# A gated MLP by seven block products: sums kept as chains in PSUM, inputs in product order, down results added by DMA

## The chip, the core and the metric

The kernel runs on one core of a Trainium2 chip. The core has five engines that run side by side, each in its own order and held back only by semaphores: TensorE (PE) for matmuls, VectorE (DVE), ScalarE (ACT), GpSimd (POOL), and SyncE (SP), which issues DMAs. PSUM, where matmuls leave their sums, has eight banks of 512 fp32 words for each of 128 partitions; SBUF holds everything else on the chip. The metric is the time of one execution on the device in microseconds (us), lower is better.

## The reference

One step of a decoder layer on 1024 prompt tokens and 8 x 4 sample tokens (1056 columns in all): a state-space head group beside a pooling head group, cross-attention to 256 memory tokens, then a gated MLP, then a final norm. The change is in the MLP alone:

```python
h = rmsnorm(x, norm_ffn)
u = h @ w_up                                   # 1024 -> 2 * 2816
u, ffn_new = causal_dwconv(ffn_buf, u, ffn_conv_w, ffn_conv_b)   # width 3, each channel by itself
g, val = jnp.split(u, [D_FF], axis=-1)
x = x + (jax.nn.silu(g) * val) @ w_down        # 2816 -> 1024
```

All is fp32. Each matmul operand is split into a high and a low part (hi = the value rounded to fp32r, lo = value minus hi), and three passes are summed: w hi by x hi, w lo by x hi, w hi by x lo.

## The kernel before

**Order.** Each engine executes its instructions in the order in which the program issues them to it, by a helper class (`InOrder`); all traced rows therefore carry that helper's line, L94 before and L93 after, and are told apart by tile names. Work that is not on TensorE's direct line is spread by generators (`background`), which are moved on one step every so many ticks; a tick comes after each block of matmuls.

**Weights.** `next_unit` hands out units of weights in a fixed list of steps. For each unit ACT makes the high part (tile `wh`) from a loaded tile (`wr` or `ws`) and DVE the low part (`wl`), about two units ahead. Weight sums for the block products (`s1`, `s2`, `s4` and one difference) are made on DVE in `ws` tiles.

**First product of the MLP.** The 44 output tiles of `w_up` form 22 pairs j (gate and value). For a pair the weights are a 2 x 2 block (a11, a12, a21, a22: two output tiles by two input halves) and the tokens are two halves of 528 columns, so that the inputs are b11, b21 (right half, made first) and b12, b22 (left half). In Winograd's form of Strassen's scheme seven products do the work of eight; their inputs are b11, b21, b22 and the sums t1 to t4. A product is 4 input tiles x 3 passes x 2 column halves of 264, 24 matmuls into an `hm` tile of two PSUM banks. Pairs 0 and 1 (`NPLAIN`) are done plainly by eight products each, four of them early (`up_rh`), while the left half's inputs are still being made. For the other 20 pairs each of the seven products has its own `hm` tile, and DVE adds it to the partial sums in SBUF (`plus`, seven adds a pair; tiles `t`, and `q` for b11's product). `hm` has three buffers; two more banks are small tiles (`ms`).

**Inputs.** `inputs_lh` makes the left half's inputs in background: norm, eight scalings, b12's and b22's parts, then for each k the four sums t1 to t4, two of these on POOL, and their low parts on DVE.

**Down projection.** Six groups of three pairs, eight output tiles each: 48 units, each of two halves of 18 matmuls, placed between the products of the next group's pairs (`DOWN_AT`: none in its first pair, one after each product in the second, one in the third). For each half SP loads the running sum from DRAM (`scr_acc`) into `q`, DVE adds the PSUM tile, SP stores it. The last four pairs' down projection comes in the tail.

Of the kernel before, what the change touches and what calls it, by code (L numbers as in the profile page):

```python
# [14 lines left out]
P = 128  # L15
# [41 lines left out]
NPLAIN = 2  # L57
# [3 lines left out]
X_EVERY = 1.3  # L61
X_ON_V = False
# [19 lines left out]
def body(ctx, tc, A):  # L82
# [38 lines left out]
    pms = ctx.enter_context(tc.tile_pool(name="pms", bufs=2, space=bass.MemoryType.PSUM))  # L121
    wide = ExitStack()
    pmm = [None]

    def psum_mode(banks):
        wide.close()
        pmm[0] = wide.enter_context(tc.tile_pool(name="pmm", bufs=6 // banks, space=bass.MemoryType.PSUM))
# [29 lines left out]
    def mstile():  # L157
        return pms.tile([P, 512], F32, tag="ms", name="ms")
# [66 lines left out]
    def paired(j, between):  # L225
# [25 lines left out]
        for n in ("a11", "s2", "s1", "s4", "a21", "a22", "a12"):  # L251
            steps.append(lambda n=n: one(n))
            plains(between.pop(0))
# [6 lines left out]
    for _ in range(2):  # L260
        plains(A["w_up"][2 * j + r, h] for j in range(NPLAIN) for r in range(2) for h in range(2))
    ffn_order = []
    for gi, (j0, j1) in enumerate(JGROUPS):
        for j in range(j0, j1):
# [5 lines left out]
            if j >= NPLAIN:  # L270
                paired(j, [[A["w_dn"][g, m] for g, m in x] for x in mids])
# [1030 lines left out]
    # The first product of the gated MLP goes by 2 x 2 blocks (output tiles of a pair, inputs by halves, tokens by  # L1302
    # halves) in Winograd's form of Strassen's seven products; here come its inputs and their sums.
# [60 lines left out]
    act = {}  # L1364
    xop = {"b11": [(t[:, rh], t[:, lh]) for t in hs[:4]], "b21": [(t[:, rh], t[:, lh]) for t in hs[4:]]}

    XP = V if X_ON_V else G
    bt = []
# [40 lines left out]
    for n in ("b12", "b22", "t1", "t2", "t3", "t4"):  # L1409
        xop[n] = []  # L1410
# [447 lines left out]
```

## Time and profile before

| | before |
|---|---|
| median of 3 runs | 1742.81 us (1742.59 to 1746.6) |
| span of the profiled execution | 1745.0 us |
| TensorE / DVE / ACT / POOL busy | 97% / 68% / 41% / 10% |
| mean granted TensorE clock | 0.991 |
| gated MLP's first block product starts, its last one ends | about 1001 us, 1683 us |
| DMA moved | 242.94 MB |

The span is the time from the first to the last instruction of one profiled execution; it is 2.2 us above the median of the timed runs. Rows of the timeline give start, duration, engine, operation, result<-operands and, in brackets, the idle time ahead of the first and what ended it. Groups of instructions give busy time and mean duration, then the idle time just ahead of them. "hm<-s,wl" is a matmul into an `hm` tile with an input tile `s` and a low weight half.

### The profile page before, as it was taken

The page shows a single profiled execution, that of the slowest core. Times are in us where ns is not written, and L with a number is a line of the kernel's source. Part 1 is how long each engine was busy: PE and PEld are TensorE (multiplying, and loading weights), DVE is VectorE, ACT ScalarE, POOL GpSimd, SP SyncE. Part 2 cuts the span into 40 slices and gives each one's busy share as a digit, 9 for nine tenths or more (in the row PEclk, how much of TensorE's full clock was granted, in tenths as well). Part 3 has the DMA queues.
Part 4 walks back from the last instruction along what each step waited for, and adds up shares of the span by engine and source line. Part 5 has one row for each costly group of instructions (what it writes and reads, how often), then busy time and mean ns, then how long its engine had stood idle before and what let it go on. Part 6 is the DMA issues. An engine that isn't in the chain of part 4 may idle for free.

```text
span 1745.0 us, 30887 instructions
## 1 busy us (share of the span) xinstructions
PE 1685.5 (97%) x12298; PEld 1614.0 (92%) x12298; DVE 1178.4 (68%) x1769; ACT 709.4 (41%) x1160; POOL 181.4 (10%) x301
## 2 busy tenths in 40 slices
PE   8799999999999989999899989999999999999998
PEld 6599998898998889999679979999999999999998
DVE  7755467766856684433653689778686868678786
ACT  6455573444440233222543456334242424233353
POOL 3400000000010210011002232001010101001010
PEclk9899999999999999999999999999999999999999
DMA  8234235554458634412745522443625263444542
GB/s 346 76 104 156 78 68 105 117 124 98 90 179 295 217 111 156 133 43 73 266 158 184 170 65 61 142 157 108 198 72 200 79 193 110 161 138 133 168 137 100
DMA packets 158495, 242.94 MB, mean 139 GB/s; under 512 B 40576, under 2 KB 77568, under 8 KB 158352
## 3 DMA queue, kind: packets, MB, share of 16 engines
q1 hardware_dynamic: 158352, 240.97, 45.0%
q8 instruction: 97, 1.59, 0.4%
q14 instruction: 46, 0.38, 0.1%
HBM read 176.81 MB, written 64.11 MB: 138 GB/s over the span
## 4 chain that ended last, share of the span: by engine, by line
PE 81%; DVE 7%; DMA 6%; ACT 3%; issue 2%; POOL 1%; SPq 0%; DVEq 0%; ACTq 0%; POOLq 0%
PE hm L94 44%; PE mm L94 28%; PE ms L94 7%; DVE s L94 4%; DMA s<-scr_acs 3%; PE mb L94 2%; DVE t L94 1%; ACT s L94 1%; DMA ld<-scr_z 1%; ACT t L94 1%; DVE wl L94 0%; DMA scr_pool<-t 0%; POOL s L94 0%; DVE q L94 0%; DMA ld<-kc 0%
## 5 line engine op out<-in xcount | busy, mean ns | idle before, releaser
L94 PE MATMUL hm<-s,wh 128*128 128x264 f32 x4160 | 679.5, 285 | 0.8 <-ACT wh L94 0.4
L94 PEld LDWEIGHTS hm<-s,wh 128*128 128x128 f32 x4160 | 578.7, 189 | 1.7 <-ACT wh L94 0.6
L94 PE MATMUL mm<-s,wh 128*128 128x352 f32 x2496 | 487.5, 329 | 0.0
L94 PE MATMUL hm<-s,wl 128*128 128x264 f32 x2080 | 425.0, 286 | 8.9 <-DVE wl L94 8.8
L94 PEld LDWEIGHTS mm<-s,wh 128*128 128x128 f32 x2496 | 413.8, 189 | 5.6 <-issue 1.8
L94 PEld LDWEIGHTS hm<-s,wl 128*128 128x128 f32 x2080 | 323.7, 189 | 10.4 <-DVE wl L94 10.4
L94 ACT ACTIVATE wh<-wr 128x512 fp32r<-128x512 f32 (+1 forms) x220 | 133.6, 607 | 443.5 <-PE mm L94 238.6
L94 PE MATMUL mm<-s,wl 128*128 128x352 f32 x1248 | 270.3, 324 | 0.0
L94 DVE TENSOR_TENSOR wl<-wr,wh 128x512 fp32r<-128x512 f32 (+1 forms) x220 | 151.2, 688 | 114.3 <-ACT wh L94 113.9
L94 PEld LDWEIGHTS mm<-s,wl 128*128 128x128 f32 x1248 | 213.5, 189 | 0.4
L94 DVE SCALAR_TENSOR_TENSOR t<-t,par 128x1104 f32<-128x1104 f32 (+4 forms) x132 | 170.4, 1297 | 31.5 <-ACT t L94 30.0
L94 ACT ACTIVATE s<-s 128x512 f32<-128x512 f32 (+5 forms) x147 | 102.9, 711 | 142.4 <-DVE s L94 78.4
L94 ACT ACTIVATE wh<-ws 128x512 fp32r<-128x512 f32 x120 | 75.7, 631 | 196.5 <-PE hm L94 186.1
L94 DVE TENSOR_TENSOR q<-hm,q 128x528 f32<-128x528 f32 x96 | 67.5, 706 | 89.4 <-DMA q<-scr_acc 61.5
L94 DVE TENSOR_TENSOR s<-s 128x512 f32<-128x512 f32 (+6 forms) x97 | 84.6, 884 | 45.4 <-ACT s L94 44.1
L94 POOL COPY fst<-t 128x2 f32<-128x2 f32 x88 | 47.4, 566 | 501.3 <-DVE t L94 487.4
L94 DVE TENSOR_TENSOR t<-hm,t 128x528 f32<-128x528 f32 x100 | 68.7, 704 | 27.4 <-PE hm L94 26.9
L94 PE MATMUL mb<-s 128*128 128x256 f32 (+2 forms) x480 | 80.9, 324 | 4.6 <-DVE s L94 4.6
L94 DVE TENSOR_TENSOR wl<-ws,wh 128x512 fp32r<-128x512 f32 x120 | 82.1, 685 | 2.6 <-ACT wh L94 2.4
L94 PEld LDWEIGHTS mb<-s 128*128 128x128 f32 x480 | 71.6, 191 | 10.6 <-DVE s L94 5.4
L94 ACT ACTIVATE t<-t,par 128x1104 f32<-128x1104 f32 (+4 forms) x60 | 74.5, 1244 | 7.6 <-DVE t L94 3.4
L94 ACT ACTIVATE s<-t 128x1024 fp32r<-128x1024 f32 (+4 forms) x78 | 49.2, 673 | 46.5 <-DVE t L94 37.0
(180 smaller groups left out, 1534.8 us busy)
## 6 DMA issues: line engine op xcount, KB each, us to landing
q<-scr_acc SPq DMA_DIRECT2D x96, 264.0 KB, 3.0
scr_acc<-q SPq DMA_DIRECT2D x96, 264.0 KB, 2.1
ws<-w_up SPq DMA_DIRECT2D x60, 256.0 KB, 2.8
wr<-w_in SPq DMA_DIRECT2D x56, 256.0 KB, 3.0
wr<-w_up SPq DMA_DIRECT2D x36, 256.0 KB, 2.9
wr<-w_dn SPq DMA_DIRECT2D x48, 192.0 KB, 2.7
s<-scr_acs SPq DMA_DIRECT2D x33, 256.0 KB, 5.6
wr<-w_mo SPq DMA_DIRECT2D x32, 256.0 KB, 2.7
```

Of the source, the lines that this page charges most:

```text
L94: i = fn(*args, **kwargs)
```

## The change

All 22 pairs go by the seven products; for the first four (`NEARLY`) the products of b11 and b21 are made early, one product each with its own tile. The products of a pair form two chains: b11, t2, t1 and b22 are added up by TensorE in one `hm` tile (`pa`), t3 and t4 in another (`pb`); only the first product of a chain clears the tile. Partial sums of a chain are copied out by ACT in two halves (`copied`), or, in the first four pairs, by a DVE add with the early product. A product now does all twelve matmuls of one column half before the other. The eight PSUM banks are four `hm` tiles during the MLP and are divided anew before it and after it. The inputs are made in the order in which the products ask for them, all on DVE and ACT. The down result is copied from PSUM by ACT and added to DRAM by an accumulating DMA that POOL issues.

```diff
-NPLAIN = 2
+NEARLY = 4
 ...
-X_EVERY = 1.3
-X_ON_V = False
+X_EVERY = 1.0
 ...
+            pmm[1] = wide.enter_context(tc.tile_pool(name="pms", bufs=small, space=bass.MemoryType.PSUM))
+        pmm[0] = wide.enter_context(
+            tc.tile_pool(name="pmm", bufs=(8 - small) // banks, space=bass.MemoryType.PSUM))
 ...
+            names = ("a11", "s2", "a21", "s1", "s4", "a22", "a12")
+            if j < NEARLY:
+                names = names[1:-1]
+            paired(j, [[A["w_dn"][g, m] for g, m in x] for x in mids], names)
 ...
+    psum_mode(2, 0)
 ...
-        for n, i in (("b12", 0), ("b22", 4)):
-            for k in range(4):
-                scaled(i + k, lh)
 ...
+        for m in (0, 4, 1, 5, 2, 6, 3, 7):
+            scaled(m, lh)
+            yield
+        t2s, w12 = [], []
         for k in range(4):
             a, b = xs[k], xs[4 + k]
-            t1, t2 = [qp.tile([P, TH], F32, tag="q", name="q") for _ in range(2)]
+            V.tensor_tensor(a[:, rh], a[:, lh], a[:, rh], op=ALU.subtract)
+            t2 = qp.tile([P, TH], F32, tag="q", name="q")
+            V.tensor_tensor(t2, b[:, lh], a[:, rh], op=ALU.subtract)
+            w = (stile(F32R), stile(F32R))
+            S.activation(w[0][:, rh], t2, AF.Copy)
+            yield
+            V.tensor_tensor(w[1][:, rh], t2, w[0][:, rh].bitcast(F32), op=ALU.subtract)
+            V.tensor_tensor(b[:, rh], b[:, rh], t2, op=ALU.subtract)
+            w12.append(w)
+            xop["t2"].append((w[0][:, rh], w[1][:, rh]))
+            yield
+        w23 = []
+        for k in range(4):
+            a, b = xs[k], xs[4 + k]
+            V.tensor_tensor(a[:, lh], b[:, lh], a[:, lh], op=ALU.subtract)
+            w = (stile(F32R), stile(F32R))
+            parts(w[0][:, rh], w[1][:, rh], a[:, lh])
+            w23.append(w)
+            xop["t3"].append((w[0][:, rh], w[1][:, rh]))
 ...
-            XP.tensor_tensor(b[:, rh], b[:, rh], t2, op=ALU.subtract)
-            XP.tensor_tensor(a[:, lh], b[:, lh], a[:, lh], op=ALU.subtract)
 ...
+    def product(name, ps, first=True):
 ...
+        for b in range(2):
             for k, (xh, xl) in enumerate(xop[name]):
                 ...
+                    PE.matmul(ps[:, b, :HB], lhsT=w[:, wc], rhs=x[:, b * HB:(b + 1) * HB],
+                              start=(first and k == 0 and pi == 0), stop=(k == 3 and pi == 2), skip_group_check=not first)
+                if k % 2:
+                    tick()
+        return ps
 ...
+    def copied(out, ps):
+        for b in range(2):
+            S.activation(out[:, b * HB:(b + 1) * HB], ps[:, b, :HB], AF.Copy)
 ...
-            S.activation(v2(pre[j][:, (lh, rh)[r]]), plain_product(r, ("b11", "b21")), AF.Copy)
+        t = pre[j] = stile()
+        copied(t[:, lh], product("b11", hmtile()))
+        plus(t[:, rh], product("b21", hmtile()), t[:, lh])
 ...
-        q = qp.tile([P, TH], F32, tag="q", name="q")
-        S.activation(v2(q), product("b11"), AF.Copy)
+        q = pre[j][:, lh] if j in pre else qp.tile([P, TH], F32, tag="q", name="q")
+        if j in pre:
+            mid()
+            pa = product("t2", hmtile())
+        else:
+            pa = product("b11", hmtile())
+            copied(q, pa)
+            mid()
+            product("t2", pa, False)
+        raws2[0] = r0 = ttile()
+
+        def partial(dst):
+            if j in pre:
+                plus(dst, pa, q)
+            else:
+                copied(dst, pa)
+
+        partial(r0[:, e1])
         mid()
-        p = product("t2")
-        r0 = ttile()
-        plus(r0[:, e1], p, q)
+        pb = product("t3", hmtile())
         mid()
-        plus(r0[:, e0], product("t1"), r0[:, e1])
+        product("t1", pa, False)
+        partial(r0[:, e0])
         mid()
-        p = product("b22")
-        r1 = ttile()
-        raws2[0], raws2[1] = r0, r1
-        plus(r1[:, e0], p, r0[:, e0])
+        plus(r0[:, e0], pb, r0[:, e0])
+        product("b22", pa, False)
+        raws2[1] = r1 = ttile()
+        partial(r1[:, e0])
         mid()
-        p = product("t3")
 ...
-        p = product("t4")
-        plus(r0[:, e1], p, r0[:, e1])
+        product("t4", pb, False)
+        plus(r0[:, e1], pb, r0[:, e1])
 ...
         for hf in range(2):
-            t = qp.tile([P, TH], F32, tag="q", name="q")
-            dma(t, scr["acc"][m, hf])
 ...
-            V.tensor_tensor(v2(t), ps[:, :, :HB], v2(t), op=ALU.add)
-            dma(scr["acc"][m, hf], t)
+            t = qp.tile([P, TH], F32, tag="q", name="q")
+            S.activation(v2(t), ps[:, :, :HB], AF.Copy)
+            G.dma_start(scr["acc"][m, hf], t, accum_op=ALU.add)
 ...
     drain()
+    psum_mode(2)
```

TensorE in pair 6, where the product of t1 ends and that of b22 begins (`hm` with its buffer's number; `wh`, `wl` are the weights; "waits" names the engine whose semaphore is waited for). Before, each product has its own tile:

```order
L94 MATMUL hm_10631<-s_10104,wh_10595 128x264 x2
L94 MATMUL hm_10631<-s_10104,wl_10597 128x264 x2
L94 MATMUL hm_10631<-s_10105,wh_10595 128x264 x2
L94 MATMUL hm_10670<-s_9799,wh_10632 128x264 [waits PE_49,Activation_49]
L94 MATMUL hm_10670<-s_9799,wh_10632 128x264
L94 MATMUL hm_10670<-s_9799,wl_10634 128x264 [waits DVE_49]
L94 MATMUL hm_10670<-s_9799,wl_10634 128x264
```

After:

```order
L93 MATMUL hm_11687<-s_9863,wh_11765 128x264
L93 MATMUL hm_11687<-s_9882,wh_11765 128x264
L93 MATMUL hm_11687<-s_9882,wl_11767 128x264
L93 MATMUL hm_11687<-s_9883,wh_11765 128x264
L93 MATMUL hm_11687<-s_9914,wh_11802 128x264 [waits Activation_49]
L93 MATMUL hm_11687<-s_9914,wl_11804 128x264 [waits DVE_49]
L93 MATMUL hm_11687<-s_9915,wh_11802 128x264
```

Before, b22's first matmul goes to another buffer and waits for its weights and for a matmul long ahead; now it goes on in the buffer of t1 (11687) and waits for an ACT instruction. Which one is seen in ACT's order at the same place (`t_11761` and `t_11863` are the pair's result tiles, `s_11795` belongs to the pair before):

```order
L93 ACTIVATE wh_11765<-ws_11608 128x512
L93 ACTIVATE t_11761<-hm_11687 128x264 [waits PE_49,Pool_49]
L93 ACTIVATE t_11761<-hm_11687 128x264
L93 ACTIVATE s_11795<-t_11720 128x1024 [waits DVE_49]
L93 ACTIVATE s_11795<-t_11720 128x32
L93 ACTIVATE wh_11802<-ws_11688 128x512
L93 ACTIVATE wh_11835<-ws_11518 128x512 [waits DMAHW1_49,PE_49]
L93 ACTIVATE t_11761<-hm_11687 128x264 [waits PE_49]
L93 ACTIVATE t_11761<-hm_11687 128x264
L93 ACTIVATE wh_11871<-ws_11548 128x512 [waits DMAHW2_49,Activation_49]
L93 ACTIVATE t_11863<-hm_11687 128x264 [waits PE_49,Pool_49]
L93 ACTIVATE t_11863<-hm_11687 128x264
```

The two copies of t1's sum stand behind the weight parts of the next two units, and the wait of the first of them is for TensorE, that is for the last matmul of t1; b22's matmul waits for the second copy.

DVE while the left half's inputs are made, before (`s`, `q` are inputs and their sums, `par` the norm's gain):

```order
L94 SCALAR_TENSOR_TENSOR s<-s,par 128x528 x2
L94 TENSOR_TENSOR q<-s 128x528
L94 TENSOR_TENSOR s<-s 128x528
L94 TENSOR_TENSOR q<-s,q 128x528
L94 TENSOR_TENSOR s<-s 128x528
L94 TENSOR_TENSOR wl<-wr,wh 128x512 x2
L94 TENSOR_TENSOR s<-q,s 128x528 x2
L94 TENSOR_TENSOR s<-s 128x528 x2
L94 TENSOR_TENSOR q<-s 128x528
L94 TENSOR_TENSOR wl<-wr,wh 128x512
L94 TENSOR_TENSOR q<-s,q 128x528
```

After, the last rows ahead of t2's low weight part, which is the row with `ws`:

```order
L93 TENSOR_TENSOR s<-q,s 128x528
L93 TENSOR_TENSOR s<-s,q 128x528
L93 TENSOR_TENSOR s<-s 128x528 x2
L93 TENSOR_TENSOR q<-s 128x528 x2
L93 TENSOR_TENSOR s<-s,q 128x528
L93 TENSOR_TENSOR s<-q,s 128x528
L93 TENSOR_TENSOR s<-hm,s 128x528
L93 TENSOR_TENSOR wl<-wr,wh 128x512
L93 TENSOR_TENSOR s<-q,s 128x528
L93 TENSOR_TENSOR s<-s,q 128x528
L93 TENSOR_TENSOR s<-s 128x528 x4
L93 TENSOR_TENSOR wl<-ws,wh 128x512
```

Between the first scaling and that row stand 34 DVE instructions: the 8 scalings, 15 steps towards t2, one more sum, 4 steps of t3's inputs, 2 adds of early products and 4 low weight parts. The 12 printed rows are the later 17 of them. Before, the low parts of single inputs come first and the sums `q` are made from then on, with a step on POOL between.

The way of the down results: DVE before, the two halves of one unit,

```order
L94 TENSOR_TENSOR wl_10912<-wr_10821,wh_10910 128x384 [waits DMAHW2_49,PE_49,Activation_49]
L94 TENSOR_TENSOR t_10847<-t_10847,t_10891 128x1104 [waits DVE_49]
L94 TENSOR_TENSOR q_10859<-hm_10861,q_10859 128x528 [waits DMAHW4_49,PE_49]
L94 TENSOR_TENSOR q_10882<-hm_10884,q_10882 128x528 [waits DMAHW5_49,PE_49]
L94 TENSOR_TENSOR s_10929<-t_10847,s_10928 128x1024 [waits Activation_49]
L94 TENSOR_TENSOR s_10929<-t_10847,s_10928 128x32 [waits Activation_49]
L94 TENSOR_TENSOR wl_10951<-ws_10735,wh_10949 128x512
```

and POOL after, in the second pair of a group:

```order
L93 DMA scr_acc_83<-q_10928 128x528 [waits DMAHW1_49,Activation_49]
L93 DMA scr_acc_83<-q_10950 128x528 [waits Activation_49]
L93 DMA scr_acc_83<-q_11007 128x528 [waits Activation_49]
L93 DMA scr_acc_83<-q_11029 128x528 [waits Activation_49]
L93 DMA scr_acc_83<-q_11089 128x528 [waits Activation_49]
L93 DMA scr_acc_83<-q_11111 128x528 [waits Activation_49]
L93 DMA scr_acc_83<-q_11175 128x528 [waits DMASW0_49,Activation_49]
L93 DMA scr_acc_83<-q_11197 128x528 [waits DMASW1_49,Activation_49]
```

DVE waited for the loaded `q` (DMAHW) and for TensorE; now POOL waits for ACT's copy, and from the ninth DMA on for the one eight places earlier (DMASW).

More of the change, by code (lines that the diff above doesn't have):

```diff
@@ L1361, in body @@
     drain()
+    psum_mode(2, 0)
     act = {}
     xop = {"b11": [(t[:, rh], t[:, lh]) for t in hs[:4]], "b21": [(t[:, rh], t[:, lh]) for t in hs[4:]]}
-    XP = V if X_ON_V else G
-    bt = []
+    for n in ("b22", "t1", "t2", "t3", "t4"):
+        xop[n] = []
     def inputs_lh():
@@ L1542, in up @@
         mid()
-        plus(r1[:, e1], product("b21"), q)
+        if j in pre:
+            S.activation(r1[:, e1], pre[j][:, rh], AF.Copy)
+        else:
+            plus(r1[:, e1], product("b21", hmtile()), q)
         ends(1)
```

104 lines of the change are left out of this document (30 added, 74 removed).

## The prediction

> **What bounds the kernel now.** I read the engines' shares first, then the chain of waits, then what TensorE did before, in and after the gated MLP.
>
> ```profile
> span 1745.0 us, 30887 instructions
> PE 1685.5 (97%) x12298; PEld 1614.0 (92%) x12298; DVE 1178.4 (68%) x1769; ACT 709.4 (41%) x1160; POOL 181.4 (10%) x301
> ```
> ```profile
> 1060.36 636.80 PE hm L94 x5178
> 1697.16 2.18 PE ms L94 x12
> ```
> ```profile
> 1061.00:1697.00 636.00, 636.00 (x5177) 635.57 (x5176) 488.73 (x674) 238.17 (x369) 69.52 (x163) 1.00 0.44 138
> ```
>
> From 1060 to 1697 us the chain is one unbroken piece of TensorE: 636.80 us for 5178 matmuls, 123.0 ns each. The window (columns: PE, weight loads, DVE, ACT, POOL, granted clock, DMA share, GB/s) agrees: PE 100% busy at clock 1.00, DVE 77%, ACT 37%. So nothing that frees DVE, ACT or SP there can shorten the stage; only fewer matmuls can, and every wait put before a matmul is added to the end. What may be won elsewhere lies in the stage's start, where TensorE waits:
>
> ```profile
> 1025.89 0.51 PE L94 MATMUL hm<-s,wl 128*128 128x264 f32 x2 [1.62 <-DVE wl L94]
> 1026.24 0.65 PE L94 MATMUL hm<-s,wh 128*128 128x264 f32 x4
> ...
> 1033.22 0.51 PE L94 MATMUL hm<-s,wl 128*128 128x264 f32 x2 [1.43 <-DVE wl L94]
> 1033.56 0.66 PE L94 MATMUL hm<-s,wh 128*128 128x264 f32 x4
> ...
> 1040.39 0.51 PE L94 MATMUL hm<-s,wl 128*128 128x264 f32 x2 [1.03 <-DVE wl L94]
> ...
> 1046.83 0.77 PE L94 MATMUL hm<-s,wl 128*128 128x264 f32 x2 [3.24 <-DVE wl L94]
> 1047.40 1.08 PE L94 MATMUL hm<-s,wh 128*128 128x264 f32 x4
> ...
> 1050.67 0.41 PE L94 MATMUL hm<-s,wl 128*128 128x264 f32 x2
> ...
> 1058.60 0.51 PE L94 MATMUL hm<-s,wh 128*128 128x264 f32 x2 [0.42 <-ACT wh L94]
> 1060.36 0.66 PE L94 MATMUL hm<-s,wl 128*128 128x264 f32 x2 [1.25 <-DVE wl L94]
> 1060.82 1.08 PE L94 MATMUL hm<-s,wh 128*128 128x264 f32 x4
> ```
>
> The bracket is the wait. They sum to 9.0 us (1.62+1.43+1.03+3.24+0.42+1.25), and behind 1046.83 and 1060.36 four matmuls take 1.08 us instead of 0.65, until the rows at 1050.67 and 1064.43 (below) are at full rate again: nearly half of 3.4 and 3.6 us is lost, some 3.4 us. So the start loses **12.4 us**. All but one wait are for a low weight half (wl), which stands on DVE behind the inputs being made.
>
> **Part 1, fewer matmuls.** Before: 8 early products, 8 plain ones, 20 pairs of seven: 156 products of 24 matmuls. After: 8 early, 4 pairs of five, 18 of seven: 154. 48 matmuls × 0.123 = **−5.9 us**, certain, since they leave a stream that is full.
>
> **Part 2, the start.** The inputs' work, before and after, by these rows:
>
> ```profile
> L94 DVE TENSOR_TENSOR s<-s 128x528 fp32r<-128x528 f32 x16 | 10.7, 701 | 0.1
> L94 DVE TENSOR_TENSOR s<-q,s 128x528 fp32r<-128x528 f32 x8 | 8.6, 1119 | 2.9 <-ACT s L94 2.9
> L94 DVE TENSOR_TENSOR q<-s,q 128x528 f32<-128x528 f32 x4 | 5.1, 1264 | 0.0
> ```
> ```profile
> 1034.83 0.68 DVE L94 TENSOR_TENSOR wl<-wr,wh 128x512 fp32r<-128x512 f32 x1
> 1035.43 2.44 DVE L94 TENSOR_TENSOR s<-q,s 128x528 fp32r<-128x528 f32 x2
> ```
> ```profile
> 1034.99 1.71 POOL L94 TENSOR_TENSOR s<-s,q 128x528 f32<-128x528 f32 x1 [0.65 <-DVE q L94]
> ```
>
> The same 528-column subtraction takes 701 ns in one group and 1119 and 1264 in two others, whose rows lie beside a POOL subtraction. With POOL out of it that stretch goes: 8 × 0.42 + 4 × 0.56 = 5.6 us of DVE, plus the 2.9 us that DVE waited. Against this DVE takes over POOL's 8 sums and drops 4 low halves (+4 × 0.62 = 2.5 us; the pitch of such rows is 0.60 to 0.62, as from 1034.83 to 1035.43), and sums weights for two more pairs. More important is what is needed first: the first Strassen product, t2, needs all 8 scaled halves and 15 of the 16 steps behind them, where the plain product needed 4 scaled halves and 4 low ones.
>
> ```profile
> 1001.42 0.71 DVE L94 TENSOR_TENSOR s<-hm,t 128x528 f32<-128x528 f32 x1 [1.76 <-PE hm L94]
> ...
> 1012.76 2.12 DVE L94 SCALAR_TENSOR_TENSOR s<-s,par 128x528 f32<-128x528 f32 x3
> ```
>
> The new change of PSUM pools makes the first MLP matmul wait for the last add from the old pool (1001.42 + 0.71): it starts at about 1002.2 instead of 1001.3, **+0.9**. The scaled halves start 0.9 later, at 1013.7. From there to t2's low weight the new order has 34 DVE instructions (the order rows in the section on the change): 34 × 0.62 = 21.1, so 1034.8. TensorE has done its eight early products, 24 × 0.123 = 2.95 each, and the norm's transposes (about 1) at 1026.7: 8.1 lost. Then t3's inputs and weights, 9 × 0.62 = 5.6 against a product of 2.95: 2.6 more; t1's 6 × 0.62 = 3.7: 0.8 more. Then four times the sum t1→b22 of an early pair, where TensorE waits for one DVE add between two products of one chain: 0.16 + 0.05 + 0.70 + 0.05 = 0.96 (last matmul's drain, handover, add, handover; rows in part 3), 3.8 in all. After: 0.9 + 11.5 + 3.8 = 16.2 against 12.4 before, **+3.8**; I keep nothing for slow clock, though a long wait may bring it. Bounds: if the waits for inputs are only half (early products' weights come in between) −2; if every DVE instruction waits on its ACT copy by as much as the 2.9 us above shows once, +4. With the clock, −6 to +10.
>
> **Part 3, the chains.** From pair 4 on ACT copies a partial sum out of a PSUM tile that the next product then goes on adding to. The copies are queued behind the product's last matmul, and the next product's first matmul behind the second copy. Where other matmuls lie between, this is hidden: b11→t2 has 11 or 36, t2→t1 13 to 36, t3→t4 48. **t1→b22 has none** in the first and third pair of each group and in the last group: 12 places (pairs 5, 6, 8, 9, 11, 12, 14, 15, 17, 18, 20, 21).
>
> ```profile
> 1184.37 1.11 ACT L94 ACTIVATE t<-t 128x1104 f32<-128x1104 f32 x1
> 1185.38 0.59 ACT L94 ACTIVATE q<-hm 128x528 f32<-128x528 f32 x1
> 1185.87 0.62 ACT L94 ACTIVATE wh<-ws 128x512 fp32r<-128x512 f32 x1
> ```
> ```profile
> L94 PE MATMUL hm<-s,wh 128*128 128x264 f32 x4160 | 679.5, 285 | 0.8 <-ACT wh L94 0.4
> ```
> ```profile
> 1686.57 0.42 ACT L94 ACTIVATE t<-t 128x272 f32<-128x272 f32 x1
> ```
> ```profile
> 1064.43 0.41 PE L94 MATMUL hm<-s,wh 128*128 128x264 f32 x2
> ```
> ```profile
> 1064.88 0.61 ACT L94 ACTIVATE t<-hm 128x528 f32<-128x528 f32 x1 [0.94 <-PE hm L94]
> ```
>
> A 528-column copy out of PSUM takes 0.59 and lets the next start 0.49 later; a 272-column one takes 0.42, so two halves about 0.32 + 0.42 = 0.74. A matmul takes 0.285 to its end against 0.123 from start to start, so 0.16 of drain comes first, and a handover from PE to ACT is 0.04 (the last matmul of a product ends at 1064.43 + 0.41 = 1064.84, ACT starts at 1064.88); I take 0.05 for the way back. Price 0.16 + 0.04 + 0.74 + 0.05 = 1.0 us, 12 places: **+12 us**. ACT has little ahead of the copies there: a weight split whose tile is long free. Bounds: 0.6 a place if the halves overlap more, 1.6 if a split (0.62) stands in the way: +7 to +19. What the chains save, four DVE adds a pair, is worth nothing: DVE was not waited for.
>
> **Part 4, down results.** Loads (96) leave SP, the adds leave DVE (96 × 0.706), both off the path. ACT copies the PSUM tile to q and POOL issues the accumulating DMA.
>
> ```profile
> q<-scr_acc SPq DMA_DIRECT2D x96, 264.0 KB, 3.0
> scr_acc<-q SPq DMA_DIRECT2D x96, 264.0 KB, 2.1
> ```
> ```profile
> L94 DVE TENSOR_TENSOR q<-hm,q 128x528 f32<-128x528 f32 x96 | 67.5, 706 | 89.4 <-DMA q<-scr_acc 61.5
> ```
>
> The trace has no accumulating DMA; it both reads and writes 264 KB, so between 2.1 and 3.0 + 2.1 = 5.1 us. In a second pair two of the three q buffers serve the downs, and a copy waits for the DMA two copies earlier. Two copies come per 36 matmuls of down and 24 of product, 60 × 0.123 = 7.4 us. Less the copy's own 0.6 that is 6.8 us for a DMA before ACT waits; TensorE fills one more hm tile meanwhile (18 matmuls, 2.2, less a copy's 0.5), so it waits above 8.5. 5.1 is below both: I cost it at **0**.
>
> **Part 5, small.** The products run one half (bank) through before the other:
>
> ```profile
> 1683.66 13.51 PE L94 MATMUL hm<-s 128*128 128x400 f32 x72
> 1728.67 1.67 PE L94 MATMUL mb<-s 128*128 128x256 f32 x12
> ```
>
> Runs into one bank at 400 columns: (13.51 − 0.16)/72 = 185 ns, 0.464 a column, 122 ns at 264: no loss. At 256 columns in the tail: (1.67 − 0.16)/12 = 126, 130 at 264: +7 ns × 154 products × 24 = +26 at worst. The first rows are many and in the same kind of tile: **+0**. The second change of pools, ahead of the 400-column matmuls, lets them wait for the last product's add, from its end near 1683.6 to
>
> ```profile
> 1684.14 0.70 DVE L94 TENSOR_TENSOR t<-hm,q 128x528 f32<-128x528 f32 x1
> ```
>
> 1684.84: **+1.2** (0 to 2).
>
> **Sum.** −5.9 + 3.8 + 12 + 0 + 0 + 1.2 = **+11.1 us**. The profiled execution is 1745.0 from first to last instruction, 2.2 above the median of the runs, 1742.81; I add the sum to the median: 1753.9, say **1754 us**. Ends: −5.9 − 6 + 7 + 0 = −5 (1738); −5.9 + 10 + 19 + 2 = +25 (1768).
>
> **Rivals.** *A, faster:* DVE's stretch beside POOL is all that the start waits for; without it no input comes late. Place: 1025 to 1060. Price: the 12.4 us go and nothing takes their place: −5.9 − 12.4 + 12 + 1.2 = −5.1, and with a place of part 3 at 0.8, between its lower bound and my value, −7.5: 1735 us. It decides from the point where t2's low weight is ready by 1026.7 instead of 1034.8. For it: the rows of 1119 and 1264 ns. Against: 23 input steps ahead of t2 where 8 were enough. 0.25. *B, within 0.3%:* the copies run beside the drain and the matmuls of the other half, 0.25 a place: −5.9 + 3.8 + 3 + 1.2 = +2, 1745. For it: the first half is complete 12 matmuls earlier. Against: the order lets both copies wait for the product's last matmul. 0.18. *C, slower by DMA:* above 8.5 us per accumulation TensorE waits for q; at 10 us, with 8 pieces of down in 6 groups, 1.5 × 8 × 6 = +72, 1826. For it: loads of scr_acc were what DVE waited for longest before its adds (61.5 us in the row above). 0.08. *D, slower by clock:* short waits make the clock fall; at the 1.7 us lost after the 3.24 wait, 16 places, +27 on the forecast, 1781. Against: after waits of 1.62 and 1.43 the next four matmuls took 0.65. 0.05. Forecast: 0.44.
>
> The Trainium skill, "TensorE: Matmul & The Clock Gate", section "A second HAM failure mode: psum-queue depth-cycling", says that frequent short idling of TensorE between matmul groups makes the clock swing between half and full rate. That speaks against this change and would make D the result; the rows after 1025.89 and 1033.22 show no such fall.
>
> **How the numbers follow.** About 0.3% (5.2 us) is what a measurement of this kernel tells from no change. Faster: 0.22 of A (its rest ends inside 0.3%) and 0.02 from the forecast's low end: 0.24. Same: 0.18 of B, 0.03 of A and 0.02 of the forecast: 0.23. Slower: the rest, 0.53. The range takes in A, B and the forecast's own ends with 5 us beyond them, and leaves out C, D and the outermost of A, under 2 in 10: **1731 to 1773**.
>
> **What would show it.** Part 1: 5424 matmuls of 264 columns in the MLP. Part 2: TensorE's waits between 1025 and 1060, named DVE wl or DVE s, 10 to 16 us, the first at t2; DVE rows of 0.70 with none above 1. Part 3: in the chain of waits, the unbroken PE piece cut at 12 places by ACT t, near 1.0 us each, none at b11→t2. Part 4: the scr_acc DMA under 6.8 us to landing, and ACT waiting for PE, not DMA, before its q copies. Wrong would be a cut every pair, ACT waiting on DMA, or a granted clock below 0.97 between 1100 and 1640.

## The result, and the profile after

The changed kernel takes **1761.47 us** (median of 4 runs, 1761.29 to 1765.65) against 1744.7 us (4 runs, 1742.59 to 1750.22) for the kernel before on the same chip. The ratio is 1.0098, 95% interval 1.0075 to 1.0122: slower by 16.8 us, about 1%, where 11 were forecast. The engines' shares of the profiled execution after:

```profile
span 1759.5 us, 30638 instructions
...
PE 1686.8 (96%) x12250; PEld 1612.8 (92%) x12250; DVE 1081.2 (61%) x1621; ACT 783.8 (45%) x1374; POOL 252.2 (14%) x389
```

TensorE does 48 matmuls less in the program, DVE is freed of 97 us, ACT has 74 us more. What was one piece of TensorE in the chain of waits is now in pieces (start, length, what):

```profile
1095.68 73.21 PE hm L93 x599
...
1169.64 6.11 PE hm L93 x48
...
1182.10 9.06 PE hm L93 x71
...
1191.90 76.34 PE hm L93 x624
...
1268.99 6.11 PE hm L93 x48
```

The waits view of TensorE, first for the start of the MLP (995 to 1102 us), then for the rest of it (1110 to 1700); the numbers are us in total, how often, the longest.

```profile
PE hm L93 <- DVE wl L93: 7.8, 3, 4.1
PE hm L93 <- DVE t L93: 4.7, 4, 1.4
PE hm L93 <- ACT wh L93: 1.5, 2, 0.8
PE hm L93 <- DVE s L93: 0.9, 1, 0.9
```

The last line of it is the first change of pools. Then:

```profile
PE hm L93 <- ACT t L93: 9.2, 12, 0.8
PE hm L93 <- DVE wl L93: 2.5, 6, 0.4
PE hm L93 <- DVE t L93: 1.3, 1, 1.3
```

This second fence is the result in three lines: twelve waits for a copy of a partial sum, six for a low weight half that the prediction did not have, one for the second change of pools. Before, this stretch had no wait at all. The windows view of nearly the same stretch (columns as before) says that nothing else happened to TensorE: it is busy 584.36 of 596.00 us, the 11.6 that are missing are these twelve and six waits (9.2 + 2.5), and the granted clock is 1.00:

```profile
1101.00:1697.00 596.00, 584.36 (x4758) 579.96 (x4756) 336.18 (x431) 291.72 (x546) 147.30 (x241) 1.00 0.50 95
```

To compare kernels I cut every trace at the starts of the same matmuls. *Ahead* runs from TensorE's first matmul to the MLP's first product; *start* ends at pair 4's first product (720 matmuls before, 672 after); *main* ends at the first 400-column matmul (4752 matmuls in all kernels); then the tail, up to the start of TensorE's last matmul. "Lost" is the time between starts of neighbouring matmuls above their usual 0.122 us, counted where the excess is 0.08 us or more; so it takes in the drain ahead of a wait, and slow matmuls: in some runs of four or more they start about 0.22 us apart.

| us | ahead | start (lost) | main (lost) | tail |
|---|---|---|---|---|
| before | 999.8 | 103.8 (16.1) | 578.6 (0) | 54.4 |
| after | 997.6 | 102.4 (20.2) | 597.0 (17.1) | 54.0 |

Main is 18.4 us longer. Its 17.1 are the twelve and the six waits; a last 1.5 is the change of pools, behind the last of its matmuls.

**The twelve.** One of them in the timeline, TensorE and then ACT (start, duration, operation, idle time and its releaser):

```profile
1190.86 0.28 PE L93 MATMUL hm<-s,wh 128*128 128x264 f32 x1
1191.90 0.39 PE L93 MATMUL hm<-s,wh 128*128 128x264 f32 x1 [0.76 <-ACT t L93]
1192.13 0.29 PE L93 MATMUL hm<-s,wl 128*128 128x264 f32 x1
```
```profile
1191.18 0.67 ACT L93 ACTIVATE t<-hm 128x264 f32<-128x264 f32 x2 [1.66 <-PE hm L93]
```

The last matmul of t1 ends at 1191.14, ACT starts 0.04 later, both copies take 0.67, and b22's first matmul starts 0.05 behind them. Start to start that is 1.04 where 0.12 is usual, and the next step is 0.23 instead of 0.12: 1.02 lost; the twelve lose 12.3 us.

**The six.** They stand near 1182, 1281, 1381, 1480, 1579 and 1678 us, between b11 and t2 of pairs 6, 9, 12, 15, 18 and 21, which have no down projection between their products. TensorE, DVE, ACT:

```profile
1182.10 0.39 PE L93 MATMUL hm<-s,wl 128*128 128x264 f32 x1 [0.41 <-DVE wl L93]
...
1183.46 0.39 PE L93 MATMUL hm<-s,wh 128*128 128x264 f32 x1
```
```profile
1178.18 1.37 DVE L93 SCALAR_TENSOR_TENSOR t<-t,par 128x1104 f32<-128x1104 f32 x1 [1.01 <-ACT t L93]
1179.46 0.70 DVE L93 TENSOR_TENSOR t<-hm,q 128x528 f32<-128x528 f32 x1
1180.08 1.36 DVE L93 SCALAR_TENSOR_TENSOR t<-t,par 128x1104 f32<-128x1104 f32 x1
1181.36 0.68 DVE L93 TENSOR_TENSOR wl<-ws,wh 128x512 fp32r<-128x512 f32 x1
```
```profile
1180.53 1.31 ACT L93 ACTIVATE t<-t,par 128x1104 f32<-128x1104 f32 x1
1181.74 1.11 ACT L93 ACTIVATE t<-t 128x1104 f32<-128x1104 f32 x1
1182.76 0.65 ACT L93 ACTIVATE q<-hm 128x264 f32<-128x264 f32 x2
```

The 1104-column rows are the convolution and its SiLU (`conv`), moved on in background. On ACT they stand ahead of the two copies of b11's sum (`q<-hm`), which are ready only at 1183.4. TensorE's list has eleven matmuls of t3 between b11 and t2, although the program writes t2 first: in the MLP `InOrder` holds no engine to the program's order (`strict` is False there), unlike what the section on the kernel before says. TensorE runs these eleven meanwhile, and t3's low weight half stands on DVE behind a convolution step. So two things are late at once. The wait that the view shows is for DVE's weight half, but t2's first matmul starts at 1183.46, 0.05 behind the copies, so a weight half in time would not have let it start earlier. Such a place loses 0.8 us, six of them 4.8.

**The rest.** The accumulating DMAs and ACT's copies ahead of them (groups of instructions, DMA issues):

```profile
scr_acc<-q POOLq DMA_DIRECT2D x96, 264.0 KB, 4.1
```
```profile
L93 ACT ACTIVATE q<-hm 128x528 f32<-128x528 f32 (+1 forms) x132 | 69.5, 540 | 49.8 <-PE hm L93 31.0
```

4.1 us from issue to landing, between the prediction's two bounds of 2.1 and 5.1; ACT waits for TensorE ahead of these copies, not for a DMA.

### The profile page after: what moved, and what is told of

Its sections match the earlier page's. It is cut to its first block, busy times and chain, and to the rows that moved or that the text cites. A ratio compares the mean times of both kernels' runs of the same rounds, so it can differ in the third digit from the quotient of the medians.

```text
span 1759.5 us, 30638 instructions
## 1 busy us (share of the span) xinstructions
PE 1686.8 (96%) x12250; PEld 1612.8 (92%) x12250; DVE 1081.2 (61%) x1621; ACT 783.8 (45%) x1374; POOL 252.2 (14%) x389
## 4 chain that ended last, share of the span: by engine, by line
PE 78%; DVE 10%; DMA 6%; ACT 3%; issue 2%; POOL 0%; SPq 0%; DVEq 0%; ACTq 0%; POOLq 0%
PE hm L93 41%; PE mm L93 29%; PE ms L93 7%; DVE s L93 4%; DVE t L93 3%; PE mb L93 2%; DMA s<-scr_acs 2%; ACT t L93 1%; ACT s L93 1%; DVE wl L93 1%; DMA ld<-scr_z 1%; DMA ld<-w_mv 1%; DVE ws L93 1%; DMA s<-xT 1%; DMA s<-w_mk 0%
## 5 line engine op out<-in xcount | busy, mean ns | idle before, releaser
L93 PE MATMUL hm<-s,wh 128*128 128x264 f32 x4128 | 730.0, 286 | 16.5 <-ACT t L93 9.2
L93 PEld LDWEIGHTS hm<-s,wh 128*128 128x128 f32 x4128 | 616.0, 189 | 21.5 <-ACT t L93 12.8
L93 PE MATMUL hm<-s,wl 128*128 128x264 f32 x2064 | 519.2, 285 | 10.3 <-DVE wl L93 10.3
L93 PEld LDWEIGHTS hm<-s,wl 128*128 128x128 f32 x2064 | 362.3, 189 | 12.2 <-DVE wl L93 12.2
L93 ACT ACTIVATE wh<-wr 128x512 fp32r<-128x512 f32 (+1 forms) x210 | 127.5, 607 | 369.8 <-PE mm L93 240.6
L93 DVE TENSOR_TENSOR wl<-wr,wh 128x512 fp32r<-128x512 f32 (+1 forms) x210 | 144.7, 690 | 170.1 <-ACT wh L93 169.8
L93 ACT ACTIVATE s<-s 128x512 f32<-128x512 f32 (+5 forms) x147 | 102.4, 711 | 132.6 <-DVE s L93 81.8
L93 POOL DMA_DIRECT2D scr_acc<-q x96 | 83.2, 866 | 218.6 <-ACT q L93 212.3
L93 DVE TENSOR_TENSOR s<-s 128x512 f32<-128x512 f32 (+7 forms) x105 | 89.4, 869 | 40.2 <-ACT s L93 38.9
L93 ACT ACTIVATE q<-hm 128x528 f32<-128x528 f32 (+1 forms) x132 | 69.5, 540 | 49.8 <-PE hm L93 31.0
L93 ACT ACTIVATE t<-hm 128x264 f32<-128x264 f32 x108 | 36.4, 389 | 114.1 <-PE hm L93 114.1
```

Source lines behind the costliest of these rows:

```text
L93: i = fn(*args, **kwargs)
```

## The experiments

All of them start from the changed kernel and compute the whole of the reference. Ratios are to the kernel before on the same chip.

**Two tiles of one bank instead of one of two (e1_halves).** A product's two column halves get PSUM tiles of their own, so the next product's first half waits for the first copy alone.

```diff
-            pa = product("b11", hmtile())
+            pa = product("b11", halves())     # [mbtile(), mbtile()], one bank each
...
-                    PE.matmul(ps[:, b, :HB], ...
+                    PE.matmul(ps[b][:, :HB], ...
...
-    psum_mode(2, 0)
+    psum_mode(1, 0)
```

> The changed kernel with every PSUM tile of the MLP split into two tiles of one bank, so that a copy or add of the first half waits for 12 matmuls only and the next product's first half waits for that copy alone (adds and copies become two of 264 columns). Theory A (the waits at t1 to b22 are handovers of a whole two-bank tile: 12 of 1.03 us, and 4 of about 1.2 us in the early pairs): all 16 go, -17 us against 1761.5, so 1744 to 1746; the six waits for a low weight half near 1182, 1281, 1380, 1479, 1579 and 1678 us stay, 0.8 us each. Rival B (ACT is late at these places, whatever the tile): the waits stay, 1757 or more.

1748.3 us, ratio 1.0012 (0.9999 to 1.0026). Main falls from 597.0 to 583.1; the chain of waits has one piece of TensorE again up to 1658 us, and the waits view from 1110 us on has one line, the second change of pools:

```profile
1100.60 557.64 PE mb L93 x4560
```
```profile
PE hm L93 <- DVE t L93: 1.4, 1, 1.4
```

All eighteen link waits are gone, and with them 13.9 us of the 17.1 lost; 26 short hesitations (starts that come 0.1 to 0.3 us late, too short for the waits view), 3.2 us, stay. So the links carry the result. The expectation had the six stay; that they went too is the first sign that they are links. This run does not tell the twelve from the six, since it takes both.

**b22 in a tile of its own (e2_own22).** The chain ends at t1; b22 is added by DVE as before.

```diff
+        raws2[1] = r1 = ttile()
+        partial(r1[:, e0])
         mid()
         plus(r0[:, e0], pb, r0[:, e0])
-        product("b22", pa, False)
-        raws2[1] = r1 = ttile()
-        partial(r1[:, e0])
+        plus(r1[:, e0], product("b22", hmtile()), r1[:, e0])
```

> The changed kernel with only the last link of the first chain undone: b22's product goes to a tile of its own, the sum up to t1 is copied twice by ACT, and DVE adds b22's tile to the second copy. Theory A: the 16 waits ahead of b22 go, -17 us, 1744 to 1746, with the other links of the chains in place and costing nothing; the waits for low weight halves stay. Rival B (ACT's load): two more copies in each pair, no gain, 1760 or more.

1758.11 us, 1.0074 (1.0047 to 1.0101). Main is 585.4, 11.6 less; the waits there:

```profile
PE hm L93 <- DVE wl L93: 2.5, 6, 0.4
PE hm L93 <- DVE t L93: 2.1, 1, 2.1
```

The twelve are gone, the six are as they were: two separate causes. The time is not the 1744 to 1746 expected. Of the sixteen waits that were to go, the four in the start are only changed for others: TensorE's waits from 995 to 1106 us sum to 14.9 as in the changed kernel. Start (105.2) and the part ahead of the MLP (1001.9) were longer in this execution, by no more than they vary between kernels (last section), so the time shows less of the gain than main does.

**One copy instead of two halves (e4_onecopy).**

```diff
-        for b in range(2):
-            S.activation(out[:, b * HB:(b + 1) * HB], ps[:, b, :HB], AF.Copy)
+        S.activation(v2(out), ps[:, :, :HB], AF.Copy)
```

> The changed kernel with a chain's sum copied by one ACT instruction of 528 columns instead of two of 264. Theory A: the wait is drain, handover and copy; two halves take 0.67 us in the trace, one takes 0.59, so 0.08 us less at 12 places: -1 us, 1760.5, the waits 0.68 instead of 0.76. Rival (the next product's first half starts after the first of the two copies, so halves are better): 1762 or more.

```profile
1178.08 0.39 PE L93 MATMUL hm<-s,wh 128*128 128x264 f32 x1 [0.70 <-ACT t L93]
```

The wait is 0.70 instead of 0.76, main 595.9 instead of 597.0: twelve times 0.06, and a little. The copy's length is in the wait, as the price of a place had it. The time, 1768.5 us (1754.84 to 1769.54; ratio 1.0117, 1.0074 to 1.0161), shows nothing of it; the profiled execution lost its time ahead of the MLP (1003.6 against 997.6) and in the start (105.0 against 102.4), of which the last section tells more.

**Halves inside, as before (e5_binner).** The loop over the two column halves goes back inside the three passes.

```diff
-        for b in range(2):
-            for k, (xh, xl) in enumerate(xop[name]):
...
-                for pi, (w, x) in enumerate(((whi, xh), (wlo, xh), (whi, xl))):
...
+        for k, (xh, xl) in enumerate(xop[name]):
...
+            for pi, (w, x) in enumerate(((whi, xh), (wlo, xh), (whi, xl))):
+                for b in range(2):
```

> The changed kernel with the two column halves of a product alternating matmul by matmul again, as before the change, instead of one half after the other. Theory A: order of halves is free, 0 within 1 us: 1761. Rival C (matmuls in a row into one bank cost more): up to -7 us, 1754.

1766.62 us, 1.0129 (1.01 to 1.0157); main 597.1, the wait unchanged:

```profile
1170.46 0.51 PE L93 MATMUL hm<-s,wh 128*128 128x264 f32 x2 [0.76 <-ACT t L93]
```

The order of the halves is worth nothing in main by itself; runs into one bank go as fast as alternating ones (0.122 us from start to start both ways).

**Down results as before (e3_plaindown).** The running sum is loaded, added on DVE and stored.

```diff
+            t = qp.tile([P, TH], F32, tag="q", name="q")
+            dma(t, scr["acc"][m, hf])
...
-            t = qp.tile([P, TH], F32, tag="q", name="q")
-            S.activation(v2(t), ps[:, :, :HB], AF.Copy)
-            G.dma_start(scr["acc"][m, hf], t, accum_op=ALU.add)
+            V.tensor_tensor(v2(t), ps[:, :, :HB], v2(t), op=ALU.add)
+            dma(scr["acc"][m, hf], t)
```

> The changed kernel with the way of the down results alone undone: SP loads q, DVE adds the PSUM tile, SP stores. Theory A (accumulating in DRAM neither costs nor saves time here): the stretch from pair 4 to the 400-column matmuls stays at 597 us within 2, DVE's 96 adds of 0.62 us lengthening the six waits for a low weight half by some tenths each: 1761 to 1764. Rival E (the accumulating DMAs and ACT's 96 copies hold up the partial sums or the weights): 585 to 592 us in that stretch, the whole below 1757.

1769.01 us, 1.0144 (1.0121 to 1.0166); main 596.9, with both kinds of wait as after:

```profile
1180.19 0.39 PE L93 MATMUL hm<-s,wh 128*128 128x264 f32 x1 [0.76 <-ACT t L93]
...
1192.65 0.39 PE L93 MATMUL hm<-s,wl 128*128 128x264 f32 x1 [0.41 <-DVE wl L93]
```

The accumulating DMA costs TensorE nothing in main, and ACT's 96 copies for it are not what makes the links late. The time is above the 1761 to 1764 expected, by what the stages ahead of main took in this kernel (last section).

**Eight input sums on POOL again (e6_pool).**

```diff
-            V.tensor_tensor(b[:, rh], b[:, rh], t2, op=ALU.subtract)
+            G.tensor_tensor(b[:, rh], b[:, rh], t2, op=ALU.subtract)
...
-            V.tensor_tensor(a[:, lh], b[:, lh], a[:, lh], op=ALU.subtract)
+            G.tensor_tensor(a[:, lh], b[:, lh], a[:, lh], op=ALU.subtract)
```

> The changed kernel with the eight sums of the inputs that were POOL's before the change back on POOL. Theory A (the start is as long as DVE's work, and a POOL subtraction stretches the DVE subtraction beside it by about as much as it takes off it: 1.1 us for 0.62): the stretch from the first MLP product to pair 4 stays at 102.4 us within 2; DVE rows of 1.8 us appear. Rival F (the eight steps were the cause of the longer start): 4 to 5 us less, 97.5 to 98.5.

1766.08 us, 1.0124 (1.0097 to 1.0152); the start grows to 106.5, longer than either expectation. POOL, DVE and TensorE there:

```profile
1025.55 1.76 POOL L93 TENSOR_TENSOR s<-s 128x528 f32<-128x528 f32 x1
1027.28 1.77 POOL L93 TENSOR_TENSOR s<-s,q 128x528 f32<-128x528 f32 x1
```
```profile
1026.08 1.78 DVE L93 TENSOR_TENSOR wl<-wr,wh 128x512 fp32r<-128x512 f32 x1
1027.79 1.81 DVE L93 TENSOR_TENSOR wl<-ws,wh 128x512 fp32r<-128x512 f32 x1
```
```profile
1027.92 0.59 PE L93 MATMUL hm<-s,wl 128*128 128x264 f32 x1 [7.16 <-DVE wl L93]
```

A low weight half that takes 0.68 alone takes 1.8 beside a POOL subtraction, and TensorE waits 7.16 at once. The stretch that the prediction read is real. Part of the longer start is something else: 50 matmuls in it, against 29 in the changed kernel, were slow, about 0.22 us from start to start instead of 0.122. Without what these runs of slow matmuls cost, 19.1 us are lost against 17.2, so taking these sums off POOL was worth about 2 us here. The Trainium skill, "SBUF — State Buffer", section "Who interferes with whom", says that a DVE instruction with two SBUF inputs contends with a GpSimd instruction that reads SBUF; these rows agree.

**Halves, with the matmuls held in program order (e7_halves_order).** In the changed kernel TensorE takes eleven matmuls of t3 ahead of t2 where b11's copies are late. This kernel is e1_halves with every matmul held behind the one before it.

```diff
+    def mm(*a, **k):
+        i = PE.matmul(*a, **k)
+        if plast[0] is not None:
+            tc.add_manual_dep(i.ins, plast[0], NOSYNC, reason="program order")
+        plast[0] = i.ins.name
...
-                    PE.matmul(ps[b][:, :HB], ...
+                    mm(ps[b][:, :HB], ...
```

> One-bank tiles as in e1_halves, and the matmuls of the MLP held to the order in which the program writes them, so that t3's first matmuls can't run ahead of t2's. Theory A (the waits for low weight halves come from t3 running ahead of t2, whose weights are made one unit earlier): the small waits left in e1_halves after pair 4 (3.2 us in all) go, 580 us from pair 4 to the 400-column matmuls instead of 583.1; 1745. Rival G (DVE is late there whatever runs first): the same 583 or more.

Longer, and not shorter as expected: 1756.39 us, 1.0069 (1.0041 to 1.0096), main 588.5. The waits view, one of the six places, and ACT at it:

```profile
PE mb L93 <- ACT q L93: 7.0, 6, 1.2
```
```profile
1188.97 0.39 PE L93 MATMUL mb<-s,wh 128*128 128x264 f32 x1 [1.17 <-ACT q L93]
```
```profile
1186.32 1.32 ACT L93 ACTIVATE t<-t,par 128x1104 f32<-128x1104 f32 x1
1187.54 1.11 ACT L93 ACTIVATE t<-t 128x1104 f32<-128x1104 f32 x1
1188.55 0.65 ACT L93 ACTIVATE q<-mb 128x264 f32<-128x264 f32 x2
```

That t3 runs ahead is not the harm, it is the remedy: without it TensorE stands until ACT has gone through the convolution and the SiLU to b11's copy. No wait for a weight half is left in main. So the six places are the link b11→t2, late by what stands ahead of its copies on ACT.

**Early products as a chain (e8_early).** As e7_halves_order, but b21 is added to b11 in PSUM for the first four pairs, two DVE adds less for each.

```diff
-        copied(t[:, lh], product("b11", halves()))
-        plus(t[:, rh], product("b21", halves()), t[:, lh])
+        ps = product("b11", halves())
+        copied(t[:, lh], ps)
+        copied(t[:, rh], product("b21", ps, False))
```

> e7_halves_order with the early products of b11 and b21 as a chain too, copied out by ACT, so that DVE makes four adds (eight of 264 columns, 2.9 us) less in the start. Theory A (the start is as long as DVE's work): the stretch from the first MLP product to pair 4 is 2 to 3 us shorter than in e7_halves_order, about 97; 1742. Rival H (the start waits for t2's inputs alone, adds of early products lie in idle time): no shorter.

1752.31 us, 1.0062 (1.0033 to 1.0091); main is 588.5 as in e7_halves_order, the start 100.5 against 104.4. The intervals of the two overlap, and the starts differ mostly by slow matmuls (22 against 57): without these 16.2 and 16.5 us are lost. So a gain is not shown, and rival H stands.

**Convolution steps one tick further apart (a9_conv5).** The changed kernel with this edit alone.

```diff
-CONV_EVERY = 4
+CONV_EVERY = 5
```

> The changed kernel with one number changed: the background steps of a pair's convolution come every 5 ticks instead of 4, so that ACT's second convolution step and the SiLU (1.3 and 1.1 us) stand behind the copies of the next pair's b11 and not ahead of them; what is computed and all dependences stay. e7_halves_order showed that without t3 running ahead the next product waits 1.45 us for these copies. Theory A' (the six waits of 0.8 us near 1182, 1281, 1380, 1479, 1579, 1678 us are the link b11 to t2, whose copies stand behind that work on ACT): they shrink to 0.2 or less, 592 to 593.5 us from pair 4 to the 400-column matmuls instead of 597.0. Rival G (DVE is short of time there, whatever ACT's order): they stay at 0.6 or more, 596 or more.

1759.73 us, 1.0086 (1.0069 to 1.0102), main 593.4. The waits in main:

```profile
PE hm L93 <- ACT t L93: 9.2, 12, 0.8
PE hm L93 <- DVE t L93: 1.3, 1, 1.3
```

The six are gone, by nothing but the place of the convolution in the queues; the twelve stand. The edit moves the convolution on both engines: b11's copies now come ahead of the SiLU on ACT (1184.08 and 1184.64), and t3's low weight half ahead of the convolution step on DVE (1182.57 and 1183.16). It is e7_halves_order, where TensorE waits for ACT's copies alone, that tells the two apart.

**Three edits together (e10_best).** One-bank tiles, early products as a chain, `CONV_EVERY = 5`; the matmuls not held.

> One-bank tiles (e1_halves), early products of b11 and b21 as one chain, and the convolution steps every 5 ticks. Theory A': nothing is left of the waits from pair 4 on but small ones, 579 to 581 us there, and 99 to 102 in the start: 3 to 6 us below the kernel before, ratio 0.997 to 0.999. Rival H (what is saved in waits comes back as DVE work in half-size adds): 583 or more, ratio 1.001.

1745.41 us against 1745.61: 0.9992 (0.9981 to 1.0002). Main 582.5, with no wait of the kinds above but the change of pools. Back at the time before, and no further.

**b21 between t1 and b22 (e12_b21mid).** With two-bank tiles and `CONV_EVERY = 5`, a product of another tile covers the copies of t1's sum, except in the last pair.

```diff
...
+        raws2[1] = r1 = ttile()
+        moved = j not in pre and j < NJ - 1
+        if moved:
+            plus(r1[:, e1], product("b21", hmtile()), q)
+            mid()
         product("b22", pa, False)
-        raws2[1] = r1 = ttile()
...
```

> Two-bank tiles as in the changed kernel, but the product of b21, which depends on no chain, is put between t1 and b22 from pair 4 to 20 (24 matmuls of cover for the copies), and the convolution steps come every 5 ticks. Theory A': 11 of the 12 waits at b22 go and the six others shrink, 581 to 583 us from pair 4 on, start unchanged: ratio 1.000 to 1.003. Rival B (ACT is late there, whatever lies between): 590 or more.

1754.63 us, 1.0049 (1.0033 to 1.0065), main 588.0 where 581 to 583 were expected:

```profile
PE hm L93 <- DVE wl L93: 4.0, 5, 0.8
PE hm L93 <- DVE t L93: 1.3, 1, 1.3
PE hm L93 <- ACT t L93: 0.8, 1, 0.8
```

Eleven of the twelve are covered by 24 matmuls between; the last pair's stays. But the new order makes five low weight halves late. At the first of them, 1201.68, the trace has DVE at work without a pause from 1191.7 on, with convolution steps, adds and three weight sums ahead of the low weight half that TensorE waits for (1200.95 to 1201.63). That another order of these would mend it was not tried.

**b11 put back into PSUM (e13_seed).** e10_best, and in the first four pairs b11's early product is split into a high and a low part and laid into the chain by 16 matmuls with the identity, so that ACT copies replace DVE adds.

```diff
-            pa = product("t2", halves())
+            pa = halves()
+            for b in range(2):
+                for i in range(2):
+                    c = i * TH + b * HB
+                    PE.matmul(pa[b][:, :HB], lhsT=one, rhs=seed[j][:, c:c + HB], start=(i == 0), stop=(i == 1))
+            product("t2", pa, False)
```

> e10_best with the early product of b11 put back into PSUM by TensorE in the first four pairs (identity times its high and low part, 4 matmuls of 264 columns a pair, 2 us in all), so that the partial sums of these pairs are copied by ACT too: 24 half-size DVE adds of 0.35 us go, 4 subtractions of 0.62 come, 6 us less for DVE in the start. Theory A (the start is as long as DVE's work): the stretch from the first MLP product to pair 4 falls from 99.1 us to 94 to 97, the rest stays at 582.5: ratio to the kernel before 0.996 to 0.9985. Rival H (the start waits for t2's and t3's inputs alone, and what comes later finds time): 99 to 101 us, ratio 0.9995 to 1.001.

1742.11 us (11 runs) against 1743.45 (15 runs): 0.9988 (0.9976 to 1.0000). The start is 97.7, the shortest of all, main 582.7. Of the 1.4 us that the start is shorter than in e10_best, 1.2 are fewer slow matmuls (26 that cost 2.9 us, against 40 that cost 4.1), so the edit itself has not shown a gain. Its median is the lowest of the versions made here; that it is faster than the kernel before is not shown.

## Why the prediction was right in sign and short in size

Its sum, term by term (us; the measured ones from the traces before and after):

| term | predicted | measured |
|---|---|---|
| 1, 48 matmuls fewer | −5.9 | −5.9 (5424 matmuls of 264 columns) |
| 2, the start | +3.8 | +5.2 (1.1 at the first change of pools; then 20.2 lost, 16.1 before) |
| 3, link t1→b22 | +12 | +12.3 |
| 3, link b11→t2 | 0 | +4.8 |
| 4, accumulating DMA | 0 | 0 |
| 5, order of halves | 0 | 0 |
| 5, second change of pools | +1.2 | +1.5 |
| sum | +11.1 | +17.9 |

The medians differ by 16.8, the profiled spans by 14.5. The difference between 17.9 and 14.5 lies mostly ahead of the MLP: with the first change of pools that part should be 1.1 longer, and in this execution it was 2.2 shorter; it varies by more than that (last section).

**The step that failed** is a sentence in part 3, "Where other matmuls lie between, this is hidden: b11→t2 has 11 or 36", which put the link b11→t2 at nothing. Its look at what ACT has ahead of the copies was for t1→b22 alone. Eleven matmuls cover 1.3 us. That is more than the 1.0 of a bare handover, but in six places the convolution and SiLU, 1.31 + 1.11 us, stand ahead of the copies; the prediction even quoted such a place of the kernel before (the SiLU at 1184.37 and the copy of `q` right behind it). In a kernel where nothing waited for that copy it cost nothing. e7_halves_order shows the link bare (1.17 of wait), a9_conv5 takes it away by moving the convolution.

**The twelve places** of t1→b22 came out at 1.02 each against 1.0, and part of that closeness is luck. Drain 0.16, handover 0.04, copies 0.67 (0.74 forecast) and way back 0.05 make 0.92; the other 0.10 is the matmul after, which starts 0.23 behind b22's first instead of 0.12 and for which the prediction had no term.

**Part 2** was near in sum but not in its places. The waits are 14.9 in all: 0.9 at the first change of pools (0.9 forecast), 4.7 at the four sums t1→b22 of the early pairs (3.8), 9.3 for weight halves (11.5 for inputs and weights). Between 1025 and 1061 us, where it expected 10 to 16, they are 9.3. The first long one is not at t2: it is for the last early product's low weight half, and t2 then finds its own ready; the second is for t3's. They stand at 1025 and 1036:

```profile
1025.33 0.39 PE L93 MATMUL hm<-s,wl 128*128 128x264 f32 x1 [3.15 <-DVE wl L93]
...
1026.35 0.64 PE L93 MATMUL hm<-s,wh 128*128 128x264 f32 x2
...
1029.64 0.40 PE L93 MATMUL hm<-s,wh 128*128 128x264 f32 x2
...
1036.91 0.59 PE L93 MATMUL hm<-s,wl 128*128 128x264 f32 x1 [4.09 <-DVE wl L93]
```

Slow matmuls follow (0.64 for two instead of 0.40) for some 3 us each, which cost about 2.9 us together and for which the prediction kept nothing. One start is a weak measure because of them: e3_plaindown has the same start, and there 53 matmuls were slow, where 29 are here, and it took 105.3 us. Without them the two lose 17.4 and 17.2 us, and the kernel before 12.9.

**The rivals.** A falls: the stretch of DVE rows beside POOL went, as A had it, and the start lost more all the same. B falls: a place cost 1.02, not 0.25; the two halves overlapped only where each has a tile of its own, and e1_halves is that case (1.0012, within 0.3%). C falls by the 4.1 us of the DMA and by e3_plaindown. D falls: the granted clock is 1.00 over main. The Trainium skill, "TensorE: Matmul & The Clock Gate", section "A second HAM failure mode: psum-queue depth-cycling", tells of a kernel in which TensorE idles briefly so often between groups of matmuls that the clock swings between half and full rate; nineteen waits of 0.41 to 1.30 us, at least 9.8 us apart, did not do it here. Short waits close together are another matter: in the kernel before, slow matmuls follow the waits of 0.42 and 1.25 us at 1058.60 and 1060.36, and in the start of e3_plaindown 15 of them follow waits of 0.80 and 1.39 us that stand 1.8 us apart. The changed kernel has such a pair at the same place, 0.76 and 1.38 us, with none behind it, and what decides it is open. What was forecast, slower by the links, is shown by e1_halves, e2_own22 and a9_conv5, which take them away together and each kind by itself.

**Where the saved matmuls went.** With every link mended (e10_best) the kernel is at the time before, though it does 48 matmuls less. Its main is 3.9 longer than before: 2.1 in 13 short hesitations, the rest at the change of pools. The start gave 4.7 (99.1 against 103.8) where the matmuls alone should give 5.9. So what the matmuls save is given back in small pieces within the stage, and whether more can be had is open. In the start the cost of the new input order is gone in e10_best: without slow matmuls it loses 13.1 us, near the 12.9 of the kernel before, where e1_halves still loses 17.5. The two differ by the chain of the early products and by the convolution's place, and no run adds one of them alone to e1_halves.

## What to carry to other kernels

A sum kept in PSUM that must also be read on its way turns each reading into a handover on TensorE's path: drain, semaphore, copy, semaphore, here 1.02 us, unless matmuls of another tile lie between or the tile is split so that each part waits for its own copy only. Cover is counted against what stands ahead of the copy in the reading engine's queue, not against the copy: an engine with 45% load still has 2.4 us in front of it at the wrong moment. Where TensorE is 100% busy, as here, adds taken off an engine that nothing waits for are worth nothing, and each new link is paid in full.

## What the runs showed that I had not expected

Main repeats within 0.2 us from kernel to kernel where an edit does not touch it (596.9, 597.0, 597.1, 597.1), but the part ahead of the MLP, which none of the edits here touches, ran from 996.0 to 1005.3 us, and the start varies with its slow matmuls. Executions of one program differ, and with them the mean granted clock: e4_onecopy took 1754.84 at 0.993 and 1768.29 to 1769.54 at 0.986 to 0.988. So the medians of e3_plaindown to e6_pool, 1766 to 1769, lie above the changed kernel's 1761 without any loss in main; an edit in one stage is better read from that stage's own length than from the total. Each kernel has one trace, so the runs don't tell how much of this goes with the execution and how much with the program. Why the clock differs from execution to execution was not tried.
